# A 192-byte gap ahead of both kinds of weight buffers instead of between them

## The chip, the cores and the metric

The kernel runs on one core of one Trainium2 chip. The metric is the time of the whole program on the device in microseconds (us). A matrix product on TensorE is two instructions: LDWEIGHTS puts a 128x128 stationary tile into the array, MATMUL then streams the moving operand past it, one column after the other. The profile counts LDWEIGHTS as PEld and MATMUL as PE; the two overlap, so the tile of the next product is read from SBUF while the stream of the present one is still being read from SBUF.

## The reference, cut to what matters

One decoder block on 256 tokens of width 2048, all in float32: a mixer (gated linear attention and causal pooling, merged by gates), a cross-attention into 256 memory tokens, and a gated MLP with a causal convolution of width 3.

```python
def reference(x, mem, ...):
    x = x + hybrid_mixer(rms_norm(x, g_mix), w_in, w_a2, b_a, g_gla, w_pool, pool_scale, w_branch, w_out)
    x = x + memory_cross_attention(rms_norm(x, g_cross), rms_norm(mem, g_mem), w_cq, w_ckv, w_co)
    x = x + conv_glu_ffn(rms_norm(x, g_ffn), w_up, conv_w, conv_b, w_down)
    return rms_norm(x, g_final)

def hybrid_mixer(h, ...):
    proj = h @ w_in                      # 2048 x 8208: q, k, v, r, a, p, gates
    ...                                  # chunked linear attention, pooling
    merged = gates[..., :D] * (o_gla @ w_branch[:1024]) + gates[..., D:] * (o_pool @ w_branch[1024:])
    return merged @ w_out

def conv_glu_ffn(h, w_up, conv_w, conv_b, w_down):
    u = causal_conv3(h @ w_up) + conv_b  # 2048 x 11264
    gate, val = split(u)
    return (silu(gate) * val) @ w_down   # 5632 x 2048
```

Nearly all of the arithmetic is in the dense products with w_in, w_branch, w_out, w_cq, w_ckv, w_co, w_up and w_down.

## The kernel before, in words

Activations are kept transposed: 128 features on the partitions, 256 tokens along the free dimension. Every float32 operand is split in two parts of type float32r, which TensorE takes in one pass: a high part (a rounded copy) and a low part (what is left). A product is then high times high, high times low and low times high. `Act` (L126) keeps both parts of a 128-feature chunk side by side, 256 columns of the high part and then 256 of the low (`both`, 512 columns; `hi`, its first 256).

`Weights` (L58) brings in a weight unit of 128 output features (up to 2048 input features) in two halves of 128x1024: SyncE's queue loads them into `raw` buffers, ScalarE copies each to a high tile `wh` and VectorE subtracts to get the low tile `wl` (both L110). `wh` tiles come from the pool `his`, `wl` tiles from `los`, five buffers each. Each unit is prepared `LOOK` = 3 units ahead of its use.

`gemm` (L311) goes through the 128x128 blocks of a unit; for each one `products` (L324) issues a pair. The first (L329) has the high block as its stationary tile and streams 512 columns, both parts of the activations; the second (L330) has the low block and streams the 256 columns of the high part. So the low block is loaded while the 512 columns stream, and the next high block while the 256 columns stream:

```python
nc.tensor.matmul(fours(ps), lhsT=wh, rhs=fours(act.both(c)), ...)                          # L329
pe["last"] = nc.tensor.matmul(fours(ps[:, 0:T]), lhsT=wl, rhs=fours(act.hi(c)), ...)       # L330
```

`fours` (L320) sets the order of the columns in a stream: four columns (16 bytes) at a time, then 64 bytes on, to the end; then the second 16 bytes of every 64, and so on. Four such steps go over 256 bytes in 16 columns.

Three places differ. In the values of the first projection (`va_unit`, L403 to L405) and of the memory (L721 to L723) the activations are the stationary tiles and the weights are streamed in plain order, 260 and 512 columns at a time: L403 and L404, L721 and L723 stream `wh`, L405 and L722 stream `wl`. In the last six units of the MLP (L913 to L926) a low block (L920) and a high block (L921) alternate, each with 256 columns; there the high tiles lie in buffers of `big` (`W.long`, L181), 192 bytes from the buffer's start.

Pools take their place in SBUF one after the other in the order in which they are opened (L146 to L153): `raw` 6 x 4096 bytes in each partition, `los` 5 x 4096, `pad1` 192, `his` 5 x 4096, `pad2` 64, `big` 29 x 4096. `big` holds all activations. All buffer sizes are multiples of 256, so modulo 256 the `wl` tiles begin where `raw` and the activations begin, and the `wh` tiles 192 bytes further; a block's step inside a tile (512 bytes) does not alter this. `pad2` makes up the gap to 256, so that `big` and the pools behind it lie where they would lie without gaps.

The order of the instructions on each engine is the order of the program's text; the Tile framework adds the semaphores.

Of the kernel before, what the change touches and what calls it, by code (L numbers as in the profile page):

```python
# [142 lines left out]
def block(ctx, tc, xT, memT, vecs, masks, wa2, wpool, w_va, w_in, w_branch, w_out, w_ckv_k, w_ckv_v, w_cq, w_co, w_up, w_down, out):  # L143
    nc = tc.nc
    PS = bass.MemoryType.PSUM
    const = ctx.enter_context(tc.tile_pool(name="const", bufs=1))  # L146
    raw = ctx.enter_context(tc.tile_pool(name="raw", bufs=6))
    los = ctx.enter_context(tc.tile_pool(name="los", bufs=5))
    pad1 = ctx.enter_context(tc.tile_pool(name="pad1", bufs=1))
    his = ctx.enter_context(tc.tile_pool(name="his", bufs=5))  # L150
    pad2 = ctx.enter_context(tc.tile_pool(name="pad2", bufs=1))
    big = ctx.enter_context(tc.tile_pool(name="big", bufs=29))
# [833 lines left out]
```

## Time and profile before

| what | us |
|---|---|
| median of 3 runs | 1677.18 |
| lowest and highest run | 1675.70, 1678.59 |
| the profiled execution | 1677.48 |
| its span, first to last instruction | 1675.7 |
| PE (MATMUL) busy in it | 1663.7 |
| PEld (LDWEIGHTS) busy | 1480.0 |
| DVE (VectorE) busy | 1228.0 |
| ACT (ScalarE) busy | 899.2 |

The times of the instructions come from the profiled execution, whose own time lies 1.8 us above its span. A MATMUL's recorded duration reaches to the end of its last column's way through the array, and the next MATMUL starts before that. So a busy PE says little about how fast it goes: what counts is the distance from one start to the next.

### The profile page before, as it was taken

The page shows a single profiled execution, that of the slowest core. Times are in us where ns is not written, and L with a number is a line of the kernel's source. Part 1 is how long each engine was busy: PE and PEld are TensorE (multiplying, and loading weights), DVE is VectorE, ACT ScalarE, POOL GpSimd, SP SyncE. Part 2 cuts the span into 40 slices and gives each one's busy share as a digit, 9 for nine tenths or more (in the row PEclk, how much of TensorE's full clock was granted, in tenths as well). Part 3 has the DMA queues.
Part 4 walks back from the last instruction along what each step waited for, and adds up shares of the span by engine and source line. Part 5 has one row for each costly group of instructions (what it writes and reads, how often), then busy time and mean ns, then how long its engine had stood idle before and what let it go on. Part 6 is the DMA issues. An engine that isn't in the chain of part 4 may idle for free.

```text
span 1675.7 us, 25994 instructions
## 1 busy us (share of the span) xinstructions
PE 1663.7 (99%) x9900; PEld 1480.0 (88%) x9900; DVE 1228.0 (73%) x1906; ACT 899.2 (54%) x1376; POOL 31.5 (2%) x137
## 2 busy tenths in 40 slices
PE   9999999999999999999999999999999999999997
PEld 8989988888888888889988888888888888888887
DVE  7688668677888855447777788886678887578876
ACT  7555456445556544445555555554355554445563
POOL 2000000000001100000000000000000000000000
PEclk9999999999999999999999999999999999999999
DMA  8665556656666666664446666666666666666663
GB/s 277 199 202 175 165 165 205 194 168 196 190 215 223 186 192 191 187 187 165 151 149 192 191 196 191 197 192 193 196 191 197 192 193 197 190 198 191 179 179 109
DMA packets 90734, 316.15 MB, mean 189 GB/s; under 512 B 10208, under 2 KB 11104, under 8 KB 90608
## 3 DMA queue, kind: packets, MB, share of 16 engines
q1 hardware_dynamic: 90464, 314.43, 59.9%
q8 instruction: 77, 1.26, 0.3%
q14 instruction: 49, 0.40, 0.1%
q10 hardware_dynamic: 144, 0.05, 0.0%
HBM read 312.35 MB, written 2.10 MB: 188 GB/s over the span
## 4 chain that ended last, share of the span: by engine, by line
PE 98%; DVE 1%; DMA 0%; issue 0%; SPq 0%; ACT 0%; DVEq 0%; ACTq 0%
PE ps_up L329 19%; PE ps_up L330 10%; PE ps_g L329 7%; PE ps_dn L329 7%; PE ps_g L330 4%; PE ps_dn L330 4%; PE ps_wo L329 3%; PE ps_wc L329 3%; PE ps_cq L329 3%; PE ps_ck L329 3%; PE br L329 3%; PE cv L722 2%; PE cv L721 2%; PE cv L723 2%; PE ps_cq L330 2%; PE ps_wc L330 2%
## 5 line engine op out<-in xcount | busy, mean ns | idle before, releaser
L110 ACT CAST wh<-raw 128x1024 fp32r<-128x1024 f32 (+3 forms) x602 | 614.6, 1023 | 681.7 <-issue 260.8
L110 DVE TENSOR_TENSOR wl<-raw,wh 128x1024 fp32r<-128x1024 f32 (+3 forms) x602 | 718.1, 1195 | 356.7 <-ACT wh L110 345.0
L329 PE MATMUL ps_up<-h,wh 128*128 128x512 f32 x1408 | 479.2, 385 | 0.0
L330 PE MATMUL ps_up<-h,wl 128*128 128x256 f32 x1408 | 387.2, 275 | 0.0
L329 PEld LDWEIGHTS ps_up<-h,wh 128*128 128x128 f32 x1408 | 264.3, 188 | 53.5
L330 PEld LDWEIGHTS ps_up<-h,wl 128*128 128x128 f32 x1408 | 263.3, 187 | 0.0
L329 PE MATMUL ps_g<-h,wh 128*128 128x512 f32 x512 | 176.3, 388 | 0.0
L329 PE MATMUL ps_dn<-ga,wh 128*128 128x512 f32 x512 | 174.2, 385 | 0.0
L330 PE MATMUL ps_g<-h,wl 128*128 128x256 f32 x512 | 140.9, 275 | 0.0
L330 PE MATMUL ps_dn<-ga,wl 128*128 128x256 f32 x512 | 140.8, 275 | 0.0
L329 PEld LDWEIGHTS ps_dn<-ga,wh 128*128 128x128 f32 x512 | 96.1, 188 | 19.5
L329 PEld LDWEIGHTS ps_g<-h,wh 128*128 128x128 f32 x512 | 96.1, 188 | 19.3 <-ACT wh L110 0.2
L330 PEld LDWEIGHTS ps_g<-h,wl 128*128 128x128 f32 x512 | 95.8, 187 | 0.3 <-issue 0.2
L330 PEld LDWEIGHTS ps_dn<-ga,wl 128*128 128x128 f32 x512 | 95.7, 187 | 0.0
L329 PE MATMUL ps_cq<-h,wh 128*128 128x512 f32 x256 | 87.9, 387 | 0.0
L329 PE MATMUL ps_wc<-oc,wh 128*128 128x512 f32 x256 | 87.6, 386 | 0.0
L329 PE MATMUL ps_ck<-me,wh 128*128 128x512 f32 x256 | 87.5, 386 | 0.0
L329 PE MATMUL ps_wo<-mg,wh 128*128 128x512 f32 x256 | 87.3, 385 | 0.0
L330 PE MATMUL ps_cq<-h,wl 128*128 128x256 f32 x256 | 70.5, 275 | 0.0
L330 PE MATMUL ps_ck<-me,wl 128*128 128x256 f32 x256 | 70.4, 275 | 0.0
L330 PE MATMUL ps_wc<-oc,wl 128*128 128x256 f32 x256 | 70.3, 275 | 0.0
L330 PE MATMUL ps_wo<-mg,wl 128*128 128x256 f32 x256 | 70.2, 275 | 0.0
(322 smaller groups left out, 2758.8 us busy)
## 6 DMA issues: line engine op xcount, KB each, us to landing
raw<-w_up SPq DMA_DIRECT2D x176, 512.0 KB, 4.3
raw<-w_in SPq DMA_DIRECT2D x112, 512.0 KB, 3.9
raw<-w_down SPq DMA_DIRECT2D x64, 512.0 KB, 3.5
raw<-w_branch SPq DMA_DIRECT2D x32, 512.0 KB, 4.3
raw<-w_out SPq DMA_DIRECT2D x32, 512.0 KB, 4.5
raw<-w_ckv_k SPq DMA_DIRECT2D x32, 512.0 KB, 3.7
raw<-w_ckv_v SPq DMA_DIRECT2D x32, 512.0 KB, 3.6
raw<-w_cq SPq DMA_DIRECT2D x32, 512.0 KB, 4.4
```

Of the source, the lines that this page charges most:

```text
L110: return self.nc.scalar.copy(hi, src), self.nc.vector.tensor_sub(lo, src, hi.bitcast(F32))
L329: nc.tensor.matmul(fours(ps), lhsT=wh, rhs=fours(act.both(c)), start=f, stop=False, skip_group_check=True)
L330: pe["last"] = nc.tensor.matmul(fours(ps[:, 0:T]), lhsT=wl, rhs=fours(act.hi(c)), start=False, stop=l, skip_group_check=True)
L721: nc.tensor.matmul(acc[t], lhsT=xh, rhs=wh, start=c == 0, stop=False)
L722: nc.tensor.matmul(acc[t], lhsT=xh, rhs=wl, start=False, stop=False)
L723: nc.tensor.matmul(acc[t], lhsT=xl, rhs=wh, start=False, stop=c == NC - 1)
```

## The change

The pool `pad1` of 192 bytes is opened ahead of `los` and no longer behind it. `los` begins 192 bytes further on; everything else keeps its address, since `his` has the same things ahead of it as before. The `wl` tiles, which began at the same place modulo 256 as the activations, now begin 192 bytes further, as the `wh` tiles do. No instruction is added, removed or moved: on PE, DVE, ACT, POOL and SP the program has the same instructions in the same order with the same waits, and only the addresses of the `wl` tiles differ.

```diff
     const = ctx.enter_context(tc.tile_pool(name="const", bufs=1))
     raw = ctx.enter_context(tc.tile_pool(name="raw", bufs=6))
+    pad1 = ctx.enter_context(tc.tile_pool(name="pad1", bufs=1))
     los = ctx.enter_context(tc.tile_pool(name="los", bufs=5))
-    pad1 = ctx.enter_context(tc.tile_pool(name="pad1", bufs=1))
     his = ctx.enter_context(tc.tile_pool(name="his", bufs=5))
     pad2 = ctx.enter_context(tc.tile_pool(name="pad2", bufs=1))
     big = ctx.enter_context(tc.tile_pool(name="big", bufs=29))
```

Four kinds of instruction use a `wl` address: the subtraction that writes the tile (L110 on DVE), the LDWEIGHTS of L330, the streams of L405 and L722, and the LDWEIGHTS of L920.

## Rows read from the trace of the kernel before

**Rows 1.** The page's first lines: span, then busy time and share of each engine.

```profile
span 1675.7 us, 25994 instructions
PE 1663.7 (99%) x9900; PEld 1480.0 (88%) x9900; DVE 1228.0 (73%) x1906; ACT 899.2 (54%) x1376; POOL 31.5 (2%) x137
```

**Rows 2.** The chain that ended last, shares of the span by engine.

```profile
PE 98%; DVE 1%; DMA 0%; issue 0%; SPq 0%; ACT 0%; DVEq 0%; ACTq 0%
```

**Rows 3.** Busy time (and count) of L329 alone: stretch, length, PE, PEld, granted clock.

```profile
0.00:1676.00 1676.00, 1441.45 (x4222) 792.51 (x4222) 1.00 0.60 189
...
960.00:1130.00 170.00, 170.00 (x501) 93.84 (x500) 1.00 0.63 194
```

**Rows 4.** Busy time of all engines (PE, PEld, DVE, ACT, POOL) in two stretches.

```profile
400.00:660.00 260.00, 259.99 (x1524) 230.36 (x1523) 204.41 (x315) 141.79 (x224) 12.95 (x15) 1.00 0.63 200
...
880.00:1600.00 720.00, 720.00 (x4238) 639.57 (x4237) 546.39 (x824) 386.09 (x556) 8.53 (x86) 1.00 0.62 192
```

**Rows 5.** Timeline of PE, up-projection, three pairs: start, duration, engine, line, operation.

```profile
999.95 0.39 PE L329 MATMUL ps_up<-h,wh 128*128 128x512 f32 x1
1000.18 0.28 PE L330 MATMUL ps_up<-h,wl 128*128 128x256 f32 x1
1000.29 0.39 PE L329 MATMUL ps_up<-h,wh 128*128 128x512 f32 x1
...
1000.97 0.39 PE L329 MATMUL ps_up<-h,wh 128*128 128x512 f32 x1
```

**Rows 6.** Timeline of PE, a tile of the r projection, three pairs.

```profile
126.14 0.38 PE L329 MATMUL ps_r<-h,wh 128*128 128x512 f32 x1
126.36 0.27 PE L330 MATMUL ps_r<-h,wl 128*128 128x256 f32 x1
...
127.14 0.38 PE L329 MATMUL ps_r<-h,wh 128*128 128x512 f32 x1
```

**Rows 7.** Timeline of PE, a tile of the gates, three pairs.

```profile
163.07 0.39 PE L329 MATMUL ps_g<-h,wh 128*128 128x512 f32 x1
163.30 0.28 PE L330 MATMUL ps_g<-h,wl 128*128 128x256 f32 x1
...
164.11 0.39 PE L329 MATMUL ps_g<-h,wh 128*128 128x512 f32 x1
```

**Rows 8.** Groups of PE by line and form: count, busy us, mean ns, idle before.

```profile
L329 PE MATMUL ps_up<-h,wh 128*128 128x512 f32 x1408 | 479.2, 385 | 0.0
L330 PE MATMUL ps_up<-h,wl 128*128 128x256 f32 x1408 | 387.2, 275 | 0.0
...
L722 PE MATMUL cv<-wl,me 128*128 128x512 f32 x128 | 51.0, 399 | 0.0
L721 PE MATMUL cv<-wh,me 128*128 128x512 f32 x128 | 50.9, 398 | 0.0
L723 PE MATMUL cv<-wh,me 128*128 128x512 f32 x128 | 50.2, 393 | 0.0
...
L405 PE MATMUL va<-wl,h 128*128 128x260 f32 x128 | 36.8, 288 | 1.3 <-DVE wl L110 1.2
L404 PE MATMUL va<-wh,h 128*128 128x260 f32 x128 | 36.5, 285 | 0.0
...
L920 PE MATMUL ps_dt<-ga,wl 128*128 128x256 f32 x66 | 15.7, 280 | 0.0
L921 PE MATMUL ps_dt<-ga,wh 128*128 128x256 f32 x66 | 15.7, 279 | 0.0
...
L926 PE MATMUL ps_dt<-ga,wh 128*128 128x256 f32 x66 | 8.4, 282 | 0.0
```

**Rows 9.** The page's row of the subtraction that makes the low tiles.

```profile
L110 DVE TENSOR_TENSOR wl<-raw,wh 128x1024 fp32r<-128x1024 f32 (+3 forms) x602 | 718.1, 1195 | 356.7 <-ACT wh L110 345.0
```

## The prediction

> **What bounds the kernel now.** I read the engine totals and the chain of waits first: PE is busy 99% of the span and 98% of the chain that ended last is PE [rows 1, 2]. There is no wait for data to shorten. From 880 to 1600 us PE is busy without a gap, 720.00 of 720.00 us, while DVE has 546 us of work and ACT 386 [rows 4]. So the time is the pace of PE, and nearly all of it is one pattern: the view of L329 by itself counts 4222 pairs of a 512-column and a 256-column product [rows 3].
>
> The timeline gives the pace, from one start to the next. In the up-projection three pairs take 1000.97 - 999.95 = 1.02 us, 340 ns a pair: 0.23 us from a 512 to its 256 and 0.11 from there to the next 512 [rows 5]. Over the long stretch of the same stage 501 pairs stand in 170.00 us, 339 to 340 ns each [rows 3]. 4222 x 0.340 = 1435.5 us, 86% of the span. The granted clock there is 1.00, so 2.4 GHz. Then 512 columns last 213.3 ns and 256 last 106.7 by the count of columns, 320 ns together. The recorded means are 385 and 275 ns [rows 8]; their difference of 110 ns is also the difference of the two distances, so a duration is the distance plus a fixed tail: with 340 = a + b and a - b = 110, a = 225 and b = 115, and the tail is 160 ns. So the 512 stream, during which the low block is loaded, is held up by 225 - 213.3 = 11.7 ns, and the 256 stream, during which the next high block is loaded, by 8.3 ns. These 20 ns a pair (84 us in all) are the only part of the time that an address could touch.
>
> The hold-up is not a fixed sum. In a tile of the r projection three pairs take 127.14 - 126.14 = 1.00 us, 333.3 ns a pair [rows 6], in a tile of the gates 164.11 - 163.07 = 1.04 us, 346.7 ns [rows 7]. These are the same instructions with the same addresses modulo 256, and PE has no idle time ahead of them. So there are three steady paces, 333.3, 340 and 346.7 ns, and they are 6.67 ns apart: 16 columns at 2.4 GHz, and just the time in which the rearranged stream goes once over 256 bytes. I read that as two readers that fall into step: where the load of a tile meets the stream, one of them waits, the wait shifts the meeting of the next pair, and after a few pairs the period has become a whole number of such turns (50, 51 or 52). What a tile settles on depends on how it was entered, too; 51 turns is by far the commonest, since the long stretch has it throughout [rows 3].
>
> **The change part by part.** Nothing is added or moved on any engine; one address changes, in four uses.
>
> *The load of the low block beside the 512 stream (4222 times).* It moves by three quarters of the 256-byte turn against the stream. No row shows such a load at 192 beyond a 512-column stream in this order, so I bound it. From below: all of the hold-up of the 512 stream goes, -11.7 ns, 4222 x 11.7 = -49 us. From above: the slowest 512-column streams in the trace are those of the memory's values in plain order, 399 ns recorded [rows 8], so 239 ns apart, 14 ns more than 225: +59 us. Between these ends the steps of the settled pace are what I expect to see: one turn a pair is 4222 x 6.67 = 28.1 us either way, two turns lie about at the ends. Which way? The high block, which is at 192 already, holds its stream up by 8.3 ns and the low one, at 0, by 11.7. If 192 were simply the cheaper place, the pair would come to 336.7 ns, which is no whole number of turns: it would settle at 333.3 or stay at 340. Against that, in the last units L921 and L926 stream the same form, the first with a low block at 0 loaded beside it, the second with a high block at 192: 279 and 282 ns [rows 8], so the place 0 is no dearer there, though a few pauses are in the second mean. And the pairs have slack: 128 columns of the tile have to be in before the 512 columns are out. I take the value nearest to the commonest row, the pace of 51 turns kept: 0 us.
>
> The Trainium skill speaks against any effect (SBUF — State Buffer, section "A bandwidth-pool intuition that's wrong (but worth ruling out)"): it gives TensorE an independent second read port for LDWEIGHTS beside that of the moving operand. By that rule the place of the tile against the stream could not matter, and the term is 0. The trace bears this out only in part: 340 ns a pair, against the 320 of the columns, says that something holds the streams up, and the three paces under the same addresses say that it isn't the address alone. I let it weigh a little for no change.
>
> *The streams of low tiles (L722, 128 times; L405, 128 times).* L722 streams a low tile at 0 beside a load from the activations at 0: 399 ns. L721 and L723 stream a high tile at 192 beside the same kind of load: 398 and 393 [rows 8]. As one of these L722 would gain 1 to 6 ns, 0.1 to 0.8 us in all. L405 against L404 is 288 to 285: up to 0.4 us. I take -0.4 us for both, and allow 1 us either way.
>
> *The load of the low block in the last units (L920, 66 times).* The three forms there lie within 3 ns [rows 8]: at most 0.2 us either way, taken as 0.
>
> *The subtraction on DVE (602 times, 1195 ns).* It writes to another place, while its two sources stay. It waits 345 us for ACT's copies [rows 9] and PE waits for it 1.2 us in all, at the start of the program [rows 8]. Were each 5% slower (36 us of DVE work in all), the 174 us that DVE is free between 880 and 1600 and the units prepared ahead cover it; without that cover it would be those 36 us. I take 0. In the tightest stretch, 400 to 660 us, DVE still has 204 us of work in 260 [rows 4].
>
> Sum: 0 - 0.4 + 0 + 0 against the profiled execution's 1677.48 us (span 1675.7), which lies 0.3 us above the median of the runs, 1677.18. I predict 1677 us.
>
> **Rivals.**
> Pairs settle one turn later, 346.7 ns: 1677 + 28 = 1705 us. Place: the 512 stream, with L330 starting about 232 ns after L329. For it: the pace exists already [rows 7]; the low and the high block would now both come at the same place of the turn, so that a meeting that the low block escapes at 0 could hit it. Against it: that pace is rare, since from 880 to 1600 us 4238 products, 2119 pairs, take 720 us, 339.8 ns each [rows 4]. It decides from 0.8 ns a pair on (4222 x 0.8 = 3.4 us, 0.2%), so already when an eighth of the pairs settle there; +9 us if a third do.
>
> Pairs settle one turn earlier, 333.3 ns: 1677 - 28 = 1649 us. For it: the pace exists too [rows 6], 8.3 against 11.7 ns, and L721 and L723 against L722. DVE and the loads would keep up: over 880 to 1600 DVE's 546 us would stand in 706. Against it: L926 against L921.
>
> The change does nothing that the reads can feel, by independent readers: 1677 us, as forecast for another reason; a trace with the same three paces in the same places would show it.
>
> **How the numbers follow.** Pace kept, for either reason: 0.36 (independent readers 0.1 of it). Later turn, wholly or in part: 0.35. Earlier turn, wholly or in part: 0.29. The three are near to each other because the trace shows each pace with the addresses of today and none with the new one. What counts as the same is 0.2%, 3.4 us, about what a measurement here can tell from no change: faster 0.29, same 0.36, slower 0.35. The range takes in one whole turn on both sides with the 1 us of the small terms, 1647 to 1707 us; it leaves out two turns (towards -49 or +59 us), to which I give some 0.1 a side. The likeliest case by itself is 1674 to 1681 us.
>
> **What would show it.** In the profile after, the group of L329 in the up-projection: 385 ns and pairs 340 ns apart if the pace is kept; 380 and 333, or 390 to 392 and 347, for the rivals. The 256 stream should stay near 275 ns, since its load and its columns keep their addresses; if it moves with the 512 stream, the two are coupled more closely than I took them to be. L722 near 393 to 398 would show that the moving tile's place counts. Wrong altogether would be: PE idle before L330 with DVE as releaser, or a pace that is no multiple of 6.67 ns.

## The result and the profile after

The changed kernel takes 1651.97 us (median of 4 runs, 1651.38 to 1653.88) against 1677.88 for the kernel before (4 runs, 1675.70 to 1679.13): a ratio of 0.9849, with a 95% interval of 0.9832 to 0.9866. It is 25.9 us faster. The profiled execution took 1651.46 us, 26.0 less than the one of before.

The first lines of the page after, and its chain, answer to [rows 1, 2]. PE still carries everything, and what the other engines do is the same work.

```profile
span 1649.7 us, 25994 instructions
...
PE 1637.8 (99%) x9900; PEld 1476.6 (90%) x9900; DVE 1227.2 (74%) x1906; ACT 899.6 (55%) x1376; POOL 31.2 (2%) x137
...
PE 98%; DMA 0%; DVE 0%; ACT 0%; SPq 0%; issue 0%; DVEq 0%; ACTq 0%
```

The view of L329 by itself over the long stretch of pairs answers to [rows 3]: 511 pairs stand in the 170 us, where 501 stood. The second line, of all engines from 880 to 1600 us, answers to [rows 4]: 4318 products in place of 4238, with PE busy throughout in both.

```profile
960.00:1130.00 170.00, 170.00 (x511) 95.72 (x511) 1.00 0.65 198
```

```profile
880.00:1600.00 720.00, 720.00 (x4318) 649.68 (x4317) 556.90 (x844) 397.83 (x575) 8.51 (x86) 1.00 0.64 196
```

The timeline of PE in the up-projection, to be read beside [rows 5]: three pairs take 1000.72 - 999.72 = 1.00 us, 333.3 ns a pair, where they took 1.02.

```profile
999.72 0.38 PE L329 MATMUL ps_up<-h,wh 128*128 128x512 f32 x1
999.94 0.27 PE L330 MATMUL ps_up<-h,wl 128*128 128x256 f32 x1
1000.05 0.38 PE L329 MATMUL ps_up<-h,wh 128*128 128x512 f32 x1
...
1000.72 0.38 PE L329 MATMUL ps_up<-h,wh 128*128 128x512 f32 x1
```

The groups of PE (mean ns after the comma), beside [rows 8]. The 512 stream of a pair went from 385 to 380 ns, the 256 stream from 275 to 274: most of the gain is in the stream beside which the low block is loaded, a little in the other, whose addresses are the same as before. The rows of L721 to L723, L405, L920 and L921 are read further below.

```profile
L329 PE MATMUL ps_up<-h,wh 128*128 128x512 f32 x1408 | 469.9, 380 | 0.0
L330 PE MATMUL ps_up<-h,wl 128*128 128x256 f32 x1408 | 385.8, 274 | 0.0
...
L721 PE MATMUL cv<-wh,me 128*128 128x512 f32 x128 | 50.6, 396 | 0.0
L722 PE MATMUL cv<-wl,me 128*128 128x512 f32 x128 | 50.6, 396 | 0.0
L723 PE MATMUL cv<-wh,me 128*128 128x512 f32 x128 | 50.6, 395 | 0.0
...
L405 PE MATMUL va<-wl,h 128*128 128x260 f32 x128 | 37.2, 291 | 1.7 <-DVE wl L110 1.6
...
L921 PE MATMUL ps_dt<-ga,wh 128*128 128x256 f32 x66 | 15.8, 279 | 0.0
L920 PE MATMUL ps_dt<-ga,wl 128*128 128x256 f32 x66 | 15.8, 279 | 0.0
```

4222 pairs at 6.67 ns would be 28.1 us; 26.0 came. One stage lost the new pace on its way. The last third of the MLP's down-projection (`ps_dl`, 120 pairs) enters at it: three pairs take 1573.38 - 1572.38 = 1.00 us.

```profile
1572.38 0.38 PE L329 MATMUL ps_dl<-ga,wh 128*128 128x512 f32 x1
...
1573.38 0.38 PE L329 MATMUL ps_dl<-ga,wh 128*128 128x512 f32 x1
```

After 18 such pairs, at 1578.4 us, TensorE's load waits 0.3 us for an activation chunk (`ga`) that VectorE has yet to finish. (PE's busy time shows no gap there, since a recorded stream reaches past the next start.) First that wait, from the view of the waits between 1578 and 1580 us, then the pairs behind it:

```profile
PEld ps_dl L329 <- DVE ga L249: 0.3, 1, 0.3
```

```profile
1600.02 0.39 PE L329 MATMUL ps_dl<-ga,wh 128*128 128x512 f32 x1
...
1600.36 0.39 PE L329 MATMUL ps_dl<-ga,wh 128*128 128x512 f32 x1
...
1600.70 0.38 PE L329 MATMUL ps_dl<-ga,wh 128*128 128x512 f32 x1
...
1601.04 0.39 PE L329 MATMUL ps_dl<-ga,wh 128*128 128x512 f32 x1
```

Three pairs now take 1601.04 - 1600.02 = 1.02 us: the old pace with the new addresses, and it stays so to the stage's end, some 100 pairs x 6.67 = 0.7 us. So with the low tiles at 192 both paces are there. The faster one is by far the commoner now, but a pause can leave a stage at the other.

Another part is at the program's start, where PE waits for the first low tiles (1.6 us now, 1.2 before) and the first pair comes 0.6 us later (56.4 against 55.8 us). The rest is in stages that gained less than 5 ns a stream: some of their tiles ran at 333.3 ns before, as one of r did [rows 6], and had nothing to gain. The mean of r's 512 streams fell by 3 ns, that of the gates' by 4. First the instructions on the tile `ps_k` of the first pairs (shortest, median and longest duration, first and last start) of after and of before, then the groups of r and of the gates, each before and after:

```profile
L329 PE MATMUL ps_k<-h,wh x64: 380/380/485, 56.4 to 79.8; 128*128 128x512 f32 x64
```

```profile
L329 PE MATMUL ps_k<-h,wh x64: 379/385/484, 55.8 to 79.5; 128*128 128x512 f32 x64
```

```profile
L329 PE MATMUL ps_r<-h,wh 128*128 128x512 f32 x128 | 43.9, 387 | 0.0
...
L329 PE MATMUL ps_r<-h,wh 128*128 128x512 f32 x128 | 43.4, 384 | 0.0
```

```profile
L329 PE MATMUL ps_g<-h,wh 128*128 128x512 f32 x512 | 176.3, 388 | 0.0
...
L329 PE MATMUL ps_g<-h,wh 128*128 128x512 f32 x512 | 173.3, 384 | 0.0
```

### The profile page after: what moved, and what is told of

Read it like the earlier page. It is cut to its first block, busy times and chain, and to the rows that moved or that the text cites. A ratio compares the mean times of both kernels' runs of the same rounds, so it can differ in the third digit from the quotient of the medians.

```text
span 1649.7 us, 25994 instructions
## 1 busy us (share of the span) xinstructions
PE 1637.8 (99%) x9900; PEld 1476.6 (90%) x9900; DVE 1227.2 (74%) x1906; ACT 899.6 (55%) x1376; POOL 31.2 (2%) x137
## 4 chain that ended last, share of the span: by engine, by line
PE 98%; DMA 0%; DVE 0%; ACT 0%; SPq 0%; issue 0%; DVEq 0%; ACTq 0%
PE ps_up L329 19%; PE ps_up L330 10%; PE ps_g L329 7%; PE ps_dn L329 7%; PE ps_g L330 4%; PE ps_dn L330 4%; PE ps_wc L329 3%; PE ps_cq L329 3%; PE ps_ck L329 3%; PE br L329 3%; PE ps_wo L329 3%; PE cv L723 2%; PE cv L722 2%; PE cv L721 2%; PE br L330 2%; PE ps_wc L330 2%
## 5 line engine op out<-in xcount | busy, mean ns | idle before, releaser
L110 ACT CAST wh<-raw 128x1024 fp32r<-128x1024 f32 (+3 forms) x602 | 613.3, 1021 | 653.9 <-issue 205.1
L110 DVE TENSOR_TENSOR wl<-raw,wh 128x1024 fp32r<-128x1024 f32 (+3 forms) x602 | 718.2, 1195 | 335.6 <-ACT wh L110 325.8
L329 PE MATMUL ps_up<-h,wh 128*128 128x512 f32 x1408 | 469.9, 380 | 0.0
L330 PE MATMUL ps_up<-h,wl 128*128 128x256 f32 x1408 | 385.8, 274 | 0.0
L329 PEld LDWEIGHTS ps_up<-h,wh 128*128 128x128 f32 x1408 | 264.3, 188 | 45.5
L330 PEld LDWEIGHTS ps_up<-h,wl 128*128 128x128 f32 x1408 | 264.3, 188 | 0.0
L329 PE MATMUL ps_g<-h,wh 128*128 128x512 f32 x512 | 173.3, 384 | 0.0
L329 PE MATMUL ps_dn<-ga,wh 128*128 128x512 f32 x512 | 170.8, 380 | 0.0
L330 PE MATMUL ps_g<-h,wl 128*128 128x256 f32 x512 | 140.3, 274 | 0.0
L330 PE MATMUL ps_dn<-ga,wl 128*128 128x256 f32 x512 | 140.3, 274 | 0.0
L329 PEld LDWEIGHTS ps_g<-h,wh 128*128 128x128 f32 x512 | 96.1, 188 | 16.9 <-ACT wh L110 0.2
L329 PEld LDWEIGHTS ps_dn<-ga,wh 128*128 128x128 f32 x512 | 96.1, 188 | 16.5
L330 PEld LDWEIGHTS ps_g<-h,wl 128*128 128x128 f32 x512 | 96.1, 188 | 0.3 <-issue 0.2
L330 PEld LDWEIGHTS ps_dn<-ga,wl 128*128 128x128 f32 x512 | 96.1, 188 | 0.0
L329 PE MATMUL ps_cq<-h,wh 128*128 128x512 f32 x256 | 86.2, 382 | 0.0
L329 PE MATMUL ps_wc<-oc,wh 128*128 128x512 f32 x256 | 85.9, 381 | 0.0
L329 PE MATMUL ps_ck<-me,wh 128*128 128x512 f32 x256 | 85.8, 381 | 0.0
L329 PE MATMUL ps_wo<-mg,wh 128*128 128x512 f32 x256 | 85.6, 381 | 0.1
L330 PE MATMUL ps_ck<-me,wl 128*128 128x256 f32 x256 | 70.1, 274 | 0.0
L330 PE MATMUL ps_cq<-h,wl 128*128 128x256 f32 x256 | 70.1, 274 | 0.0
L330 PE MATMUL ps_wo<-mg,wl 128*128 128x256 f32 x256 | 70.0, 274 | 0.0
L330 PE MATMUL ps_wc<-oc,wl 128*128 128x256 f32 x256 | 70.0, 274 | 0.0
```

What stands on the lines that cost most here:

```text
L110: return self.nc.scalar.copy(hi, src), self.nc.vector.tensor_sub(lo, src, hi.bitcast(F32))
```

## Experiments

All are single profiled executions beside one run of the kernel before on the same chip (1677.49 to 1679.87 us). "Low" and "high" are the places of the two kinds of tile beyond the activations, modulo 256 bytes. The third column is the count of pairs that start in the same 170 us of the trace, 960 to 1130 us; 501 is 340 ns a pair, 511 is 333. A pool more or less moves the lines of a kernel: what is L329 here is L325 or L330 in some of the timelines.

| low | high | pairs in 170 us | us |
|---|---|---|---|
| 0 | 192 (before) | 501 | 1677.48 |
| 192 | 192 (after) | 511 | 1651.46 |
| 0 | 0 | 496 | 1682.07 |
| 64 | 192 | 501 | 1675.71 |
| 128 | 192 | 501 | 1676.72 |
| 224 | 192 | 502 | 1676.15 |
| 192 | 0 | 511 | 1655.88 |
| 192 | 128 | 503 | 1669.65 |
| 192 | 160 | 501 | 1678.44 |
| 192 | 224 | 504 | 1668.70 |
| 192 by the activations' place | 192 | 511 | 1652.87 |
| 192, another 256 away | 192 | 511 | 1650.91 |

**Is it TensorE's load, or VectorE's writing?** The kernel before, with one word changed.

```diff
-            pe["last"] = nc.tensor.matmul(fours(ps[:, 0:T]), lhsT=wl, rhs=fours(act.hi(c)), ...)
+            pe["last"] = nc.tensor.matmul(fours(ps[:, 0:T]), lhsT=wh, rhs=fours(act.hi(c)), ...)
```

> The kernel before, but the second product of each pair takes the high block as its stationary tile too, so that the part high activations times low weights is left out (replaced). The low tiles are still made and written at place 0, but TensorE does not read them in the pairs: the load beside the 512 stream now comes from 192. Theory A (TensorE's load is what the change touched): pairs at 333.3 ns, about 1650 us. Rival C (where VectorE writes the low tiles is what the change touched): 340 ns, 1677 us.

Measured 1650.62 us against 1678.33. The view of L329 over the long stretch and the timeline of the pair, whose second product now names `wh`:

```profile
960.00:1130.00 170.00, 170.00 (x511) 95.72 (x511) 1.00 0.66 198
```

```profile
999.75 0.38 PE L329 MATMUL ps_up<-h,wh 128*128 128x512 f32 x1
999.97 0.27 PE L330 MATMUL ps_up<-h,wh 128*128 128x256 f32 x1
1000.08 0.38 PE L329 MATMUL ps_up<-h,wh 128*128 128x512 f32 x1
```

VectorE still wrote all low tiles to place 0, and the pace was that of the changed kernel. So the write is out, rival C falls, and the load of the tile beside the 512 stream is what the change touched. No pool had moved either. Here the same block is loaded twice, which could be a reason of its own; the run with the activations 64 bytes later (below) loads both blocks, has VectorE write the low tiles where the kernel before has them, and shows the same pace.

**Which place for the low tile?** The gap ahead of `los` is 0, 64, 128 or 224 bytes; the gaps behind it are made so that the high tiles lie at 192 (at 0 in the first).

```diff
-    pad1 = ...                                 # 192, between los and his
+    pad1 = ...  ; los = ...                    # 64, 128 or 224, ahead of los
+    pad2 = ...  ; his = ...                    # the rest up to 192 (224: up to 256 + 192)
```

> No gap at all: low and high tiles both begin where the activations begin (0, 0 modulo 256). Theory A (192 is the cheaper place for the load of a tile beside a stream, whichever tile): both loads are now at the dear place, pairs at 340 ns or a turn more, 346.7 ns, 1677 to 1705 us. Rival B (what counts is that both kinds lie alike): pairs at 333.3 ns, 1650 us, as in the changed kernel.

Measured 1682.07 us: 3.7 us slower than its kernel before. Rival B falls; that both kinds lie alike is not enough. The timeline shows how a pace that is no whole turn comes about: pairs of 0.33 and 0.36 us take turns, 0.69 for the two (999.93 to 1000.62 and again to 1001.30).

```profile
999.93 0.38 PE L325 MATMUL ps_up<-h,wh 128*128 128x512 f32 x1
...
1000.26 0.40 PE L325 MATMUL ps_up<-h,wh 128*128 128x512 f32 x1
...
1000.62 0.38 PE L325 MATMUL ps_up<-h,wh 128*128 128x512 f32 x1
...
1000.95 0.40 PE L325 MATMUL ps_up<-h,wh 128*128 128x512 f32 x1
...
1001.30 0.38 PE L325 MATMUL ps_up<-h,wh 128*128 128x512 f32 x1
```

> Low tiles 64 bytes beyond the activations, high tiles at 192. Theory A1 (only the place 0 is dear, any other does): pairs at 333.3 ns, 1650 us. Theory A2 (192 is the one good place of the 256-byte turn): pairs at 340 ns or 346.7, 1677 to 1705 us.

> Low tiles 128 bytes beyond the activations, high tiles at 192. Theory A1 (only 0 is dear): pairs at 333.3 ns, 1650 us. Theory A2 (192 alone is good): 340 or 346.7 ns, 1677 to 1705 us.

Measured 1675.71 and 1676.72 us, 501 pairs in both: theory A2, 192 is the good one of the four places tried so far. With 128 the pairs go round in fours of unequal length (0.35, 0.33, 0.34 and 0.34 us below), and yet four of them take 1001.30 - 999.94 = 1.36 us, 340 ns each, a whole number of turns for the round.

```profile
999.94 0.39 PE L330 MATMUL ps_up<-h,wh 128*128 128x512 f32 x1
...
1000.29 0.39 PE L330 MATMUL ps_up<-h,wh 128*128 128x512 f32 x1
...
1000.62 0.39 PE L330 MATMUL ps_up<-h,wh 128*128 128x512 f32 x1
...
1000.96 0.38 PE L330 MATMUL ps_up<-h,wh 128*128 128x512 f32 x1
...
1001.30 0.39 PE L330 MATMUL ps_up<-h,wh 128*128 128x512 f32 x1
```

> Low tiles 32 bytes past the good place: 224, high tiles at 192. If the place counts in steps of 64 bytes (224 lies in the same 64 as 192): 333.3 ns, about 1652 us. If it counts finer, the pace may be another: 340 ns, 1677 us, or a still shorter one.

Measured 1676.15 us, 502 pairs: 32 bytes past 192 the gain is gone. The place counts finer than 64 bytes.

**Which place for the high tile, with the low one at 192?**

```diff
     pad1 = ...  ; los = ...                    # 192
+    pad2 = ...  ; his = ...                    # so that high is at 0, 128, 160 or 224
```

> Low tiles 192 beyond the activations, high tiles at 0: the changed kernel with the high tiles' gap taken away. If the low tile's place alone is worth a turn: 3.3 ns above the changed kernel's pairs as no gap stood 3.4 ns above the kernel before, 336.7 ns, about 1665 us. If the pair of 192 with 192 is needed: 340 ns or more, 1677 to 1682 us.

Measured 1655.88 us, between the kernels and nearer to the changed one: neither number that was expected. In the long stretch 511 pairs, the good pace, so the high tile may lie at 0 there. In some other stages it is not reached, or not to the end. The groups of the memory's keys (`ps_ck`), this kernel's and then those of the changed one:

```profile
L329 PE MATMUL ps_ck<-me,wh 128*128 128x512 f32 x256 | 87.8, 389 | 0.0
```

```profile
L329 PE MATMUL ps_ck<-me,wh 128*128 128x512 f32 x256 | 85.8, 381 | 0.0
```

> Low tiles at 192, high tiles at 128. By the theory that 192 is the one good place for each kind: 340 ns, about 1677 us. If the high tile's place hardly counts as long as it is not 0: 333.3 ns, about 1652 us.

> Low tiles as in the changed kernel, high tiles 32 bytes further, at 224. If the high tile's load, too, is sensitive within 64 bytes: a pace between 333.3 and 340 ns, 1660 to 1677 us. If only the low tile's place is: 333.3 ns, 1652 us. A shorter pace than 333.3 would beat the changed kernel: 326.7 ns, about 1624 us.

> Low tiles as in the changed kernel, high tiles 32 bytes nearer, at 160. As for 224: a pace between 333.3 and 340 ns, 1660 to 1677 us, if the high tile's load is sensitive within 64 bytes; 333.3 ns, 1652 us, if only the low tile's place is; 326.7 ns, about 1624 us, if this place is better.

Measured 1669.65, 1668.70 and 1678.44 us, with 503, 504 and 501 pairs. So the high tile's place counts as well, and by 32 bytes: 128 and 224 leave about a third of the gain (7.8 and 9.2 us below their kernel before), 160 nothing. In the long stretch the paces of 503 and 504 pairs come about as rounds again: the unequal distances repeat after eight pairs with high at 128 and after seven with high at 224. Below are the starts of two pairs ten rounds apart, 80 pairs in 27.07 us and 70 in 23.67. A round is 2707 ns and 2367 ns, 406 and 355 times 6.67.

```profile
1200.06 0.38 PE L330 MATMUL ps_dn<-ga,wh 128*128 128x512 f32 x1
...
1227.13 0.38 PE L330 MATMUL ps_up<-h,wh 128*128 128x512 f32 x1
```

```profile
1200.24 0.38 PE L330 MATMUL ps_dn<-ga,wh 128*128 128x512 f32 x1
...
1223.91 0.38 PE L330 MATMUL ps_up<-h,wh 128*128 128x512 f32 x1
```

Is it a sum of two prices, one for the place of each kind? Only 0 and 192 were tried in all four combinations. In whole times these four add up: low at 192 is worth 26 us with high at 192 and with high at 0 (1682.07 to 1655.88). In the long stretch they do not: the high tile at 0 costs five pairs beside a low tile at 0 (501 to 496) and none beside one at 192. For the other places no run shows it, since each was tried with 192 for the other kind alone.

**Is it the distance, and modulo what?** Two ways to the same distances from other addresses: the activations 64 bytes later and no gap at the weights, and a further 256 bytes between the two kinds.

```diff
     los = ...
-    pad1 = ...                                 # 192
     his = ...
-    pad2 = ...                                 # 64
+    pad1 = ...                                 # 64, ahead of big; 192 behind it
     big = ...
```

> No gap ahead of the weight buffers; instead the activations' pool starts 64 bytes later, so that both low and high tiles lie 192 beyond the activations modulo 256, as in the changed kernel, but at other absolute addresses. Theory A (the distance between tile and stream modulo 256 sets the pace): pairs at 333.3 ns, about 1652 us. Rival D (the tiles' own address counts): as without gaps, 340 and 343 ns, 1677 to 1682 us.

```diff
     pad1 = ...  ; los = ...                    # 192
+    pad2 = ...                                 # 256
     his = ...
```

> Low and high tiles both 192 beyond the activations modulo 256, as in the changed kernel, but a further gap of 256 bytes between the two kinds puts the low tiles at 192 modulo 512, where the changed kernel has them at 448; the high tiles stay at 448. If the place counts modulo 256: 333.3 ns a pair, about 1652 us. If it counts modulo 512 or more: another pace, 338 to 340 ns, 1669 to 1677 us; then the run with low at 192 and high at 128, whose low tiles lay at 192 modulo 512 too, was slow for this and not for its high tiles.

Measured 1652.87 and 1650.91 us, 511 pairs in both. Rival D falls: for the pace of the long stretch the tiles' own addresses do not matter, their distance from the activations does, and 256 bytes more make no difference. The 1.4 us by which the first is slower than the changed kernel lie in one stage, `ps_wc`, which settles at the old pace there: first its group in that run, then in the changed kernel. The distances are the same in both; that the entry into the stage decides here, as in `ps_dl`, is likely but not shown.

```profile
L329 PE MATMUL ps_wc<-oc,wh 128*128 128x512 f32 x256 | 87.4, 386 | 0.0
...
L329 PE MATMUL ps_wc<-oc,wh 128*128 128x512 f32 x256 | 85.9, 381 | 0.0
```

The second also clears the run with high at 128, whose low tiles lay at 192 modulo 512: that was slow for its high tiles. It is no faster than the changed kernel beyond what single runs tell apart (1651.38 to 1653.88), and no place tried here gave more than 192 for both.

**Where do the 6.67 ns come from?** The changed kernel with the columns of a stream in plain order.

```diff
-        return ap.rearrange("p (l u e) -> p u l e", u=4, e=4)
+        return ap
```

> The changed kernel with the columns of both streams of a pair in plain order instead of 16 bytes in every 64. If the 6.67 ns come from the stream's walk over 256 bytes in 16 columns: the plain stream needs 64 columns for 256 bytes, and the paces are multiples of 26.7 ns (346.7 or 373.3 ns a pair, 1705 us and more). If 6.67 ns is a beat that is there whatever the order of the stream: a pace, or a short cycle of paces, that is a multiple of 6.67 ns and not of 26.7, near the sum that the plain streams cost elsewhere (238 and 120 ns, 358 a pair, 1754 us).

Measured 1731.30 us, 51 us slower than its kernel before. The timeline of three pairs:

```profile
1100.12 0.40 PE L329 MATMUL ps_up<-h,wh 128*128 128x512 f32 x1
...
1100.48 0.39 PE L329 MATMUL ps_up<-h,wh 128*128 128x512 f32 x1
...
1100.83 0.40 PE L329 MATMUL ps_up<-h,wh 128*128 128x512 f32 x1
...
1101.18 0.40 PE L329 MATMUL ps_up<-h,wh 128*128 128x512 f32 x1
```

Unequal pairs again, 1.06 us for three, 353.3 ns each: 53 times 6.67 and no multiple of 26.7. So the beat is not the rearranged stream's walk over 256 bytes. It is there in plain order too. Why plain order is slower stays open: `fours` sets the order in which the results are written to `ps` as well as that in which the activations are read, and no other place was tried with plain order.

## Why the prediction was right in part and wrong in its choice

*What bounds the kernel.* Right: PE's pace, 4222 pairs, and no other engine set the time. DVE's subtraction cost nothing, as forecast: 1195 ns then [rows 9] and now, and from 880 to 1600 us TensorE waits for no low tile.

```profile
L110 DVE TENSOR_TENSOR wl<-raw,wh 128x1024 fp32r<-128x1024 f32 (+3 forms) x602 | 718.2, 1195 | 335.6 <-ACT wh L110 325.8
```

*Three paces in steps of 6.67 ns, and the change as a move by one step.* Right, and the size too: the rival of the earlier turn gave 1649 us, 1652 came. It was the rival and not the forecast. That 1652 lies in the range at all is owed to the range's width, a whole turn either way; the forecast itself was no change, and of the three ways the text gave the one that came the least, 0.29. That the entry counts beside the address held too: after the change `ps_dl` shows both paces in one stage.

*The step that failed* is the choice inside the main term, "the value nearest to the commonest row, the pace of 51 turns kept: 0 us". It measured -26 us of the 28.1 that one turn is worth. Two arguments led there, and both were bad. The first was that L921, with a low block at 0 loaded beside it, was no slower than L926 with a high block at 192. These streams have other lengths and another order of columns than the pairs, and after the change L921 is at 279 ns as before, with its load at 192: in that stage the place simply says nothing about the pairs. The second was the slack of the load in the 512 stream. There is slack in time, but the stream was held up by 11.7 ns all the same, so slack did not protect it. The argument that pointed the right way, that the tile at 192 held its stream up by 8.3 ns and the one at 0 by 11.7, and that 336.7 is no whole turn, stood in the text and was given too little. It is not the mechanism either: with the low tile at 192 the high tile gives the same pace at 0 as at 192 (511 pairs both times), so 192 is not the cheaper place as such. And the hold-up is not each stream's own. By the prediction's working, 380 and 274 ns and 333.3 ns a pair make 219.7 and 113.7 ns, hold-ups of 6.4 and 7.0: the 256 stream, whose load and columns kept their addresses, lost 1 to 2 ns of its 8.3.

*The rule of independent readers.* The Trainium skill (SBUF — State Buffer, section "A bandwidth-pool intuition that's wrong (but worth ruling out)") gives LDWEIGHTS a read port of its own. Here the measurement differs: with nothing but that load changed, from the low block at 0 to the high block at 192, the time went from 1678.33 to 1650.62 us. Two ports there may be, but the two reads are not independent in time. I gave the rule a tenth; it deserved less, since the 340 ns against 320 already spoke against it.

*The reading of 6.67 ns* as the time of the stream's walk over 256 bytes fell with the plain order. The beat stays, its cause does not: no run here shows it.

*The rival of the later turn* expected that both kinds at one place of the turn would hit. With both at 0 it did get worse, 343 ns a pair (0.69 us for two); at 192 it did not.

*The streams of low tiles.* L722 went from 399 to 396 ns and L723 from 393 to 395: with L721 at 396 the three came closer together, and the sum of the means went from 1190 to 1187, 0.4 us over 128 rounds. That is the forecast's -0.4, though not by L722 alone. L405 gained nothing (288 to 291 ns, with 0.4 us more of waiting ahead of it); L404, whose tile kept its place, went from 285 to 287. L920 kept within 1 ns.

*What stays open:* why 192 is the good place for a low tile, why the high tile's best places among those tried are 0 and 192, what beats at 6.67 ns, and which entries lead to which pace. Distances other than those in the table, among them all that are no multiple of 32 bytes, were not tried.

## What to carry to other kernels

Where PE is busy all the time and yet takes more per product than its columns, compare start-to-start distances, not durations: a few ns in each of thousands of pairs was 26 us here, and the same instructions at two paces within one trace say that there is something to win. Then try the distance between the stationary tiles and the streamed operand modulo 256 bytes, each kind of tile by itself and both together, in steps of 32; the neighbours of a good place can be bad. Look at the pace of every stage, since a pause can leave one at the old pace. A comparison from another stage with other streams does not tell the direction; a run does.

## What the runs showed of the hardware

The loads of the tiles and the streams beside them disturb each other in a way that depends on their distance: moving the low tiles or the activations changed the pace (340 to 333.3 ns a pair), 256 bytes more between the tiles did not (1650.91 us). Neither DMA, VectorE nor ScalarE shows in it: over 170 us in which all three work, the 511 pairs keep 333 ns. The paces fall in with a beat of 6.67 ns, 16 columns at 2.4 GHz (the granted clock is 1.00 in these stretches): 333.3 and 340 ns a pair, or short rounds that add up to a multiple (on average 343 ns a pair over two, 340 over four, 338 over eight and over seven, and 353.3 over three in plain order). The distance does not decide alone: with the same one, `ps_dl` went from 333.3 to 340 ns a pair behind a pause of 0.3 us. The order of the columns can matter more than the place: plain order, with the places of the changed kernel, took 80 us more (1731.30 against 1651.46).
